# Three seven-product chunks in each up projection, with weight sums formed by adding transfers

## The chip, the cores and the metric

The kernel runs on one core of one Trainium2 chip. The metric is the device time of one execution in microseconds (us). A core has TensorE (PE in the profile, with its weight load as PEld), VectorE (DVE), ScalarE (ACT), GpSimd (POOL) and SyncE (SP), and 16 DMA engines that move data between the chip's main memory and the core's. SP and POOL issue most transfers here, each from a queue of its own that works strictly in order.

## The reference, cut to what matters

A decoder trunk of two layers on one sequence of 256 tokens, width 1024, in fp32. Each layer is half a SwiGLU, a token mixer, and another half SwiGLU; the mixers (delta and retention heads, then dilated and differential attention) are not touched by the change.

```
def swiglu(h, w_up, w_down):                    # w_up (1024, 5632), w_down (2816, 1024)
    gate, up = jnp.split(h @ w_up, 2, axis=-1)
    return (jax.nn.silu(gate) * up) @ w_down

for i in range(2):
    x = x + 0.5 * swiglu(rmsnorm(x, n1), wu1, wd1)
    x = x + mixer_i(rmsnorm(x, mix_norm[i]))
    x = x + 0.5 * swiglu(rmsnorm(x, n2), wu2, wd2)
return rmsnorm(x, final_norm)
```

So there are four feed-forward stages, each with an up projection and a down projection.

## The kernel before, in words

**Three products for one.** Every matrix operand is split into a rounded high part and the rest (`hi`, `lo`), and each matmul is done three times (hi·hi, hi·lo, lo·hi; `mm3`, lines 320 to 323). A weight reaches PE in blocks of 128 x 1024 numbers, 512 KB: `feed` (line 198) loads one from main memory on SP's queue, ACT casts it to `hi` (line 219), DVE subtracts to get `lo` (line 220). `feed` is called for at most four blocks ahead of the one that PE is at (`LOOKAHEAD`), and there are five buffers each for `w`, `hi` and `lo`.

**Chunks.** An up projection is cut into six chunks of columns: chunks 0 to 4 have 512 columns of the gate half and the same 512 of the up half, chunk 5 has 256 of each. The token axis has two halves t of 128, the inner axis eight k-tiles. A chunk done directly takes 8 blocks and 96 matmuls of 128x512, 12 to a block.

**Seven products.** Chunks 1 and 3 are done by the Strassen-Winograd scheme: inner axis and tokens are halved on one side, inner axis and the gate and up halves on the other, and seven products (P1 to P7) of quarter size stand for eight. Each product takes two blocks (p = 0, 1) of 6 matmuls, so a chunk takes 14 blocks and 84 matmuls. The sums of the inputs are formed once in each stage (`sums`); the sums of weights are formed for each chunk. With a, b, c, d for the weight quarters (0,0), (0,1), (1,0), (1,1), they are t = a+b, u = t+d, b+d, and u+c; in the up projection all four are DVE additions (`form`, line 180), two of each. The quarters stay in ten buffers named `raw`. Chunk 1 is interleaved with chunk 2 done directly, chunk 3 with chunk 4 (`PAIRS`, the list `SEVEN`, and `seven_and`): a product's two blocks of 6 matmuls, then mostly two blocks of 12. Chunks 0 and 5 are direct, at the two ends.

**The down projection** does its first eight k-tiles by seven products too, interleaved with the other 14 k-tiles of its first column half (`DOWN`, `seven_down`); the second column half of those 14 follows directly. Here t and b+d are formed while loading: a plain transfer of one quarter on SP (line 170), and then a transfer on POOL's queue that adds the other quarter to it in place (line 172, `accum_op`). Such a transfer is called an adding transfer below.

**What sets the order.** The program is written block by block; the framework then fixes an order of instructions for each engine, which the engine keeps. A `w` or `raw` load waits until the last reader of its buffer is done, and everything behind it on SP waits with it. In `feed`, loads of `raw` quarters are called a number of blocks ahead of their use (`LEAD`, `EARLY`).

Of the kernel before, what the change touches and what calls it, by code (L numbers as in the profile page):

```python
# [26 lines left out]
H = 4  # L27
# [8 lines left out]
LEAD, EARLY, RAW_BUFS = 4, 8, 10  # L36
# [4 lines left out]
PAIRS = ((1, 2), (3, 4))  # L41
# [4 lines left out]
def trunk(ctx, tc, a, out):  # L46
# [44 lines left out]
    def seven(w, cols, n, order, early=False, **between):  # L91

        kb = BLK // n

        def quarter(i, j, p):
            r0 = (4 * i + kb * p) * P
            return w[r0:r0 + kb * P, cols[j]:cols[j] + n].rearrange("(k p) c -> p k c", p=P)

        st = {}
        r = []  # L100
        for x in order:
            if x[0] == "P":
# [5 lines left out]
    def seven_up(w, c, mate):
        def cols(c):
            return (c * CW, FF + c * CW)  # L110

        gate, up = (cut([one(w, 0, 8, x)]) for x in cols(mate))
        return seven(w, cols(c), CW, SEVEN, G=gate, U=up)

    def up_runs(w, first=False):
        r, c = [], 0
        while c < 5:
            mate = dict(PAIRS).get(c)
            if mate is None:
                g, u = c * CW, FF + c * CW  # L120
                r += cut(([one(w, 0, 1, g), one(w, 1, 1, g), one(w, 2, 6, g)] if first and c == 0 else
                          [one(w, 0, 8, g)]) + [one(w, 0, 8, u)])
                c += 1
            else:
                r += seven_up(w, c, mate)
                c = mate + 1
        return r + cut([(0, 8, CW, [(w, 5 * CW, 256), (w, FF + 5 * CW, 256)])])
# [17 lines left out]
    stream = (up_runs(a["l0_ffn1_w_up"], True) + down_runs(a["l0_ffn1_w_down"])  # L145
              + cut(in0_runs(a["l0_w_in"]) + out_runs(a["l0_w_out"], 4))
              + up_runs(a["l0_ffn2_w_up"]) + down_runs(a["l0_ffn2_w_down"])
              + up_runs(a["l1_ffn1_w_up"]) + down_runs(a["l1_ffn1_w_down"])
              + cut(in1_runs(a["l1_w_in"]) + out_runs(a["l1_w_out"], 4))
              + up_runs(a["l1_ffn2_w_up"]) + down_runs(a["l1_ffn2_w_down"]))  # L150
# [7 lines left out]
    def load(x, p, st, quarter, n, early):  # L158
# [6 lines left out]
        if early:  # L165

            for nm, *src in {"P1": (("a", (0, 0)),), "P6": (("t", (0, 1), (0, 0)), ("d", (1, 1))),
                             "P7": (("b", (0, 1), (1, 1)),), "P2": (("c", (1, 0)),)}.get(x, ()):
                v = raw(nm + str(p)).rearrange("p (k n) -> p k n", n=n)
                nc.sync.dma_start(out=v, in_=quarter(*src[0], p))  # L170
                if src[1:]:
                    nc.gpsimd.dma_start(out=v, in_=quarter(*src[1], p), accum_op=ALU.add)
            return
        for nm, i, j in {"P1": (("a", 0, 0),), "P6": (("b", 0, 1), ("d", 1, 1)), "P2": (("c", 1, 0),)}.get(x, ()):
            nc.sync.dma_start(out=raw(nm + str(p)).rearrange("p (k n) -> p k n", n=n), in_=quarter(i, j, p))

    def form(x, p, st, early):

        def add(out, in0, in1):
            nc.vector.tensor_tensor(out=out, in0=in0, in1=in1, op=ALU.add)  # L180
# [17 lines left out]
    def feed():  # L198
        i = pos[1]
        while loaded[0] < len(stream) and loaded[0] <= i + (EARLY if stream[loaded[0]][-1] is True else LEAD):  # L200
            if isinstance(stream[loaded[0]][0], str):
                if spool[0] is None:
                    break
                load(*stream[loaded[0]])
            loaded[0] += 1
# [1121 lines left out]
```

## Time and profile before

| | us |
|---|---|
| runs | 1011.33, 1010.08, 1007.51 (median 1010.08) |
| the profiled execution | 1007.63 |
| its span, first to last instruction | 1005.8 |
| PE busy in it | 985.9 (98%) |
| DVE busy in it | 880.1 (88%) |
| ACT busy in it | 609.0 (61%) |
| third feed-forward stage, up projection (529.34 to 649.06) | 119.72 |
| the same, down projection (649.06 to 708.64) | 59.58 |

Busy shares are of the whole span. Matmuls are pipelined, so the duration of one (0.39 us) is longer than the distance to the next; the distances between starts tell the pace. The share of the DMA engines is the time that packets took, summed over 16 engines, and goes a little over 1 where packets overlap.

### The profile page before, as it was taken

What the parts mean: (1) busy time and instruction counts of PE and PEld (TensorE: products, weight loads), DVE (VectorE), ACT (ScalarE), POOL (GpSimd) and SP (SyncE); (2) the same over time, 40 slices, a digit from 0 to 9 for tenths busy, and PEclk for the clock granted to TensorE, in tenths of its full rate; (3) what the DMA queues carried; (4) which work ended last, traced back from release to release, by engine and by line L of the source; (5) the groups of instructions that cost most, each with busy time, mean ns of one, the idle gap of its engine ahead of it and who ended that gap; (6) DMA issues with size and microseconds to landing.
All of it is one profiled execution on the core that took longest, in us unless ns stands there. A gap on an engine that the chain in (4) does not pass through costs nothing.

```text
span 1005.8 us, 13951 instructions
## 1 busy us (share of the span) xinstructions
PE 985.9 (98%) x5076; PEld 812.9 (81%) x5076; DVE 880.1 (88%) x1191; ACT 609.0 (61%) x829; POOL 48.9 (5%) x56
## 2 busy tenths in 40 slices
PE   7999999999999999999999999999999999999997
PEld 6788878888777888888788888878877888888785
DVE  6999999679997699999979899998679879999994
ACT  6576666579543566666656566656556556666562
POOL 0000100100001000000000000100100000001000
PEclk9999999999999999999999999999999999999999
DMA  9665963765403577499267747935752566749731
GB/s 321 228 228 180 291 200 128 238 171 149 141 12 110 156 259 245 124 277 267 84 212 270 248 144 241 292 101 188 232 168 88 167 210 209 248 150 289 230 106 62
DMA packets 104708, 192.69 MB, mean 192 GB/s; under 512 B 6560, under 2 KB 16944, under 8 KB 104640
## 3 DMA queue, kind: packets, MB, share of 16 engines
q1 hardware_dynamic: 98752, 179.89, 55.1%
q0 software_dynamic: 5312, 11.30, 5.6%
q8 instruction: 40, 0.66, 0.3%
q10 hardware_dynamic: 576, 0.61, 0.2%
q14 instruction: 28, 0.23, 0.1%
HBM read 190.73 MB, written 1.05 MB: 191 GB/s over the span
## 4 chain that ended last, share of the span: by engine, by line
PE 89%; DVE 5%; ACT 2%; issue 1%; DMA 1%; POOL 1%; SPq 0%; POOLq 0%; ACTq 0%; DVEq 0%
PE p L322 7%; PE p L323 7%; PE p L321 7%; PE y L321 6%; PE y L323 6%; PE y L322 6%; PE gate L323 6%; PE gate L321 6%; PE gate L322 6%; PE up L321 4%; PE up L322 4%; PE up L323 4%; PE ca L321 2%; PE ca L322 2%; PE ca L323 2%; PE gtr L452 2%
## 5 line engine op out<-in xcount | busy, mean ns | idle before, releaser
L220 DVE TENSOR_TENSOR lo<-w,hi 128x1024 fp32r<-128x1024 f32 (+2 forms) x238 | 284.5, 1210 | 65.0 <-ACT hi L219 64.6
L219 ACT CAST hi<-w 128x1024 fp32r<-128x1024 f32 (+2 forms) x238 | 245.5, 1044 | 128.7 <-PE y L323 50.7
L219 ACT CAST hi<-raw 128x1024 fp32r<-128x1024 f32 x168 | 174.4, 1053 | 132.2 <-DVE raw L180 49.5
L220 DVE TENSOR_TENSOR lo<-raw,hi 128x1024 fp32r<-128x1024 f32 x168 | 201.6, 1218 | 15.4 <-ACT hi L219 14.0
L321 PE MATMUL gate<-hi,xT_hi 128*128 128x512 f32 x256 | 101.3, 400 | 2.1 <-ACT xT_hi L278 1.9
L323 PE MATMUL gate<-hi,xT_lo 128*128 128x512 f32 x256 | 101.0, 395 | 0.0
L322 PE MATMUL gate<-lo,xT_hi 128*128 128x512 f32 x256 | 100.7, 393 | 0.0
L180 DVE TENSOR_TENSOR raw<-raw 128x1024 f32<-128x1024 f32 x80 | 97.0, 1216 | 0.3
L321 PE MATMUL y<-hi,gT_hi 128*128 128x512 f32 x224 | 87.2, 392 | 1.8 <-ACT hi L219 1.8
L323 PE MATMUL y<-hi,gT_lo 128*128 128x512 f32 x224 | 87.4, 390 | 0.0
L322 PE MATMUL y<-lo,gT_hi 128*128 128x512 f32 x224 | 87.2, 389 | 0.0
L321 PE MATMUL p<-hi,fhP 128*128 128x512 f32 x192 | 75.2, 392 | 0.2
L322 PE MATMUL p<-lo,fhP 128*128 128x512 f32 x192 | 74.9, 390 | 0.1
L323 PE MATMUL p<-hi,flP 128*128 128x512 f32 x192 | 74.7, 389 | 0.0
L321 PE MATMUL up<-hi,xT_hi 128*128 128x512 f32 x192 | 74.7, 389 | 0.0
L322 PE MATMUL up<-lo,xT_hi 128*128 128x512 f32 x192 | 74.7, 389 | 0.0
L323 PE MATMUL up<-hi,xT_lo 128*128 128x512 f32 x192 | 74.7, 389 | 0.0
L321 PEld LDWEIGHTS gate<-hi,xT_hi 128*128 128x128 f32 x256 | 48.5, 190 | 12.3 <-ACT xT_hi L278 2.3
L323 PEld LDWEIGHTS gate<-hi,xT_lo 128*128 128x128 f32 x256 | 48.6, 190 | 10.3
L322 PEld LDWEIGHTS gate<-lo,xT_hi 128*128 128x128 f32 x256 | 48.7, 190 | 9.7
L321 PEld LDWEIGHTS y<-hi,gT_hi 128*128 128x128 f32 x224 | 41.7, 188 | 11.2 <-ACT hi L219 3.0
L323 PEld LDWEIGHTS y<-hi,gT_lo 128*128 128x128 f32 x224 | 42.1, 188 | 8.7
(322 smaller groups left out, 1868.0 us busy)
## 6 DMA issues: line engine op xcount, KB each, us to landing
w<-l_ffn_w_up SPq DMA_DIRECT2D x95, 512.0 KB, 4.2
raw<-l_ffn_w_up SPq DMA_DIRECT2D x64, 512.0 KB, 4.9
w<-l_ffn_w_down SPq DMA_DIRECT2D x56, 512.0 KB, 5.1
w<-l_w_in SPq DMA_DIRECT2D x50, 512.0 KB, 3.8
raw<-l_ffn_w_down SPq DMA_DIRECT2D x40, 512.0 KB, 6.5
w<-l_ffn_w_up SPq DMA_DIRECT2D x34, 256.0 KB, 4.8
raw<-l_ffn_w_down POOLq DMA_DIRECT2D x16, 512.0 KB, 9.9
w<-l_w_out SPq DMA_DIRECT2D x16, 512.0 KB, 3.6
```

What stands on the lines that cost most here:

```text
L180: nc.vector.tensor_tensor(out=out, in0=in0, in1=in1, op=ALU.add)
L219: nc.scalar.copy(out=hi[:, :k * n], in_=w[:, :k * n])
L220: nc.vector.tensor_tensor(out=lo[:, :k * n], in0=w[:, :k * n], in1=hi[:, :k * n].bitcast(F32), op=ALU.subtract)
L321: nc.tensor.matmul(ps, lhsT=xh, rhs=wh, start=start, stop=False, skip_group_check=more)
L322: nc.tensor.matmul(ps, lhsT=xh, rhs=wl, start=False, stop=False, skip_group_check=more)
L323: nc.tensor.matmul(ps, lhsT=xl, rhs=wh, start=False, stop=stop, skip_group_check=more)
L452: nc.tensor.transpose(ps[:, j * P:(j + 1) * P], gs[t][:, j * P:(j + 1) * P], ident)
```

## The change

Chunk 4 of each up projection, direct until now, is done by seven products as chunks 1 and 3 are; chunk 2 is cut into its gate half and its up half, and these and chunk 5 stand between the products of the three seven-product chunks, one block (M0 to M3) at a time: the gate half of chunk 2 in chunk 1, its up half in chunk 3, chunk 5 in chunk 4. Of the four weight sums three are now made by adding transfers in all seven-product chunks, up and down: t and b+d as in the down projection before, and u+c by a transfer that adds c to the buffer of u once P6's low part is made from it. Only u = t+d stays on DVE. The products' order changes (P3 before P7, both before P2), with the sums of the results rearranged to match. A block's own `w` load now comes ahead of the `raw` loads called with it, at most two `raw` loads are called with a block, and they are called 5 to 9 blocks ahead.

```
-PAIRS = ((1, 2), (3, 4))
+TRIPLE = ((1, "gate"), (3, "up"), (4, "last"))
+MATE, LAST = 2, 5
-LEAD, EARLY, RAW_BUFS = 4, 8, 10
+LEAD, RAW_BUFS = {"P1": 8, "P2": 5}, 10
-    SEVEN = ("P1", "G0", "G1", "P6", "G2", "G3", "P7", "U0", "U1", "P5", "U2", "U3", "P2", "P4", "P3")
-    DOWN = ("H0", "H1", "P1", "H2", "P6", "H3", "P7", "H4", "P5", "P2", "H5", "P4", "P3", "H6")
+    SEVEN = ("P1", "M0", "P6", "M1", "P5", "M2", "P3", "P7", "M3", "P2", "P4")
+    DOWN = ("H0", "H1", "P1", "H2", "P6", "H3", "P5", "H4", "P3", "P7", "H5", "P2", "P4", "H6")
...
-    def load(x, p, st, quarter, n, early):
+    def load(x, p, st, quarter, n):
...
+        for nm, *src in {"P1": (("a", (0, 0)),), "P6": (("t", (0, 1), (0, 0)), ("d", (1, 1))),
+                         "P7": (("b", (0, 1), (1, 1)),), "P2": (("c", (1, 0)),)}.get(x, ()):
+            v = raw(nm + str(p)).rearrange("p (k n) -> p k n", n=n)
+            nc.sync.dma_start(out=v, in_=quarter(*src[0], p))
+            if src[1:]:
+                nc.gpsimd.dma_start(out=v, in_=quarter(*src[1], p), accum_op=ALU.add)
...
         if x == "P6":
-            if not early:
-                st[f"t{p}"] = g["t"] = new()
-                add(g["t"], g["a"], g["b"])
             st[f"u{p}"] = g["u"] = new()
-            add(g["u"], g["t"], g["d"])
-        elif x == "P7" and not early:
-            add(g["b"], g["b"], g["d"])
-        elif x == "P4":
-            add(g["u"], g["u"], g["c"])
+            nc.vector.tensor_tensor(out=g["u"], in0=g["t"], in1=g["d"], op=ALU.add)
...
+        some = 0
+        while loaded[0] < len(stream) and loaded[0] <= i + LEAD.get(stream[loaded[0]][0], 9):
+            if isinstance(stream[loaded[0]][0], str):
+                if spool[0] is None or loaded[0] >= ends[0] or some == 2:
+                    break
+                some += 1
+                load(*stream[loaded[0]])
+            loaded[0] += 1
...
+        if stream[i][0] == "P6":
+            nc.gpsimd.dma_start(out=w.rearrange("p (k n) -> p k n", n=n), in_=stream[i][3](1, 0, stream[i][1]),
+                                accum_op=ALU.add)
...
-            while c < 6:
...
+            xs_run(gate, xT_hi, xT_lo, 0, 8)
+            xs_run(up, xT_hi, xT_lo, 0, 8)
+            chunk_out(0, gate, up, CW)
+            finish(sm)
+            for c, mate in TRIPLE:
+                seven_and(c, mate)
```

What this does to the order is shown at three places, all in the third feed-forward stage.

SP's queue from chunk 0 to the second seven-product chunk, before. `w` rows are blocks of chunks done directly, `raw` rows quarters of a seven-product chunk.

```order
L218 DMA w_5197<-l_ffn_w_up 128x2x512
L175 DMA raw<-l_ffn_w_up 128x2x512 x2
L218 DMA w_5215<-l_ffn_w_up 128x2x512
L218 DMA w_5291<-l_ffn_w_up 128x2x512
L175 DMA raw<-l_ffn_w_up 128x2x512 x4
L218 DMA w_5309<-l_ffn_w_up 128x2x512
L218 DMA w_5350<-l_ffn_w_up 128x2x512
L218 DMA w_5368<-l_ffn_w_up 128x2x512
L218 DMA w_5418<-l_ffn_w_up 128x2x512
L175 DMA raw<-l_ffn_w_up 128x2x512 x2
```

The same place after the change; w_5277 is M0 of chunk 1, w_5347, w_5401 and w_5481 are M1 to M3, and w_5575, w_5630, w_5684, w_5764 are M0 to M3 of chunk 3.

```order
L186 DMA w_5277<-l_ffn_w_up 128x2x512
L160 DMA raw<-l_ffn_w_up 128x2x512 x8
L186 DMA w_5347<-l_ffn_w_up 128x2x512
L186 DMA w_5401<-l_ffn_w_up 128x2x512
L186 DMA w_5481<-l_ffn_w_up 128x2x512
L186 DMA w_5575<-l_ffn_w_up 128x2x512
L160 DMA raw<-l_ffn_w_up 128x2x512
L186 DMA w_5630<-l_ffn_w_up 128x2x512
L160 DMA raw<-l_ffn_w_up 128x2x512
L186 DMA w_5684<-l_ffn_w_up 128x2x512
L160 DMA raw<-l_ffn_w_up 128x2x512 x2
L186 DMA w_5764<-l_ffn_w_up 128x2x512
```

Eight `raw` loads in one go (a, t, d, b, two of each) take the place of two and four, the rows behind them are c and then a of the next chunk, and the next row after the last one shown is `raw` x4: t and d of chunk 3, two of each.

POOL's queue in the third stage, before and then after; the rstd row is the reciprocal root of the stage's norm, L162 are the adding transfers into t and b, L203 those into u.

```order
L286 TENSOR_TENSOR rstd_3461<-rsq,mhalf 128x2
L172 DMA raw<-l_ffn_w_down 128x2x512 x4
L1055 DMA lamv<-lamv 128x256
```

```order
L270 TENSOR_TENSOR rstd_3500<-rsq,mhalf 128x2
L162 DMA raw<-l_ffn_w_up 128x2x512 x4
L203 DMA raw<-l_ffn_w_up 128x2x512 x2
L162 DMA raw<-l_ffn_w_up 128x2x512 x4
L203 DMA raw<-l_ffn_w_up 128x2x512 x2
L162 DMA raw<-l_ffn_w_up 128x2x512 x4
L203 DMA raw<-l_ffn_w_up 128x2x512 x2
L162 DMA raw<-l_ffn_w_down 128x2x512 x4
L203 DMA raw<-l_ffn_w_down 128x2x512 x2
L1036 DMA lamv<-lamv 128x256
```

Four adding transfers in a stage become 24, 18 of them in the up projection.

DVE's queue where the first seven-product chunk ends and the second begins, before: lo_5619 is chunk 1's last product, lo_5633 and the one behind w_5664 belong to chunk 3 and its companion.

```order
L220 TENSOR_TENSOR lo_5619<-raw,hi_5618 128x1024
L441 SCALAR_TENSOR_TENSOR g<-q,rstd_3461,s 128x512
L441 SCALAR_TENSOR_TENSOR g<-r,rstd_3461,s 128x512
L180 TENSOR_TENSOR raw<-raw 128x1024
L276 TENSOR_TENSOR gT_lo<-gtr,gT_hi 128x4x128
L180 TENSOR_TENSOR raw<-raw 128x1024
L276 TENSOR_TENSOR gT_lo<-gtr,gT_hi 128x4x128
L180 TENSOR_TENSOR raw<-raw 128x1024
L220 TENSOR_TENSOR lo_5633<-raw,hi_5632 128x1024
L220 TENSOR_TENSOR lo_5663<-w_5664,hi_5662 128x1024
```

The same place after: lo_5530 is the last block of chunk 1 (P4), lo_5550 and lo_5560 are the two blocks of P1 of chunk 3, lo_5574 is its M0, lo_5589 and lo_5616 are P6.

```order
L200 TENSOR_TENSOR lo_5519<-raw,hi_5518 128x1024
L416 TENSOR_TENSOR r<-r,p_5329 128x512
L200 TENSOR_TENSOR lo_5530<-raw,hi_5529 128x1024
L172 TENSOR_TENSOR raw<-raw 128x1024 x2
L200 TENSOR_TENSOR lo_5550<-raw,hi_5549 128x1024
L200 TENSOR_TENSOR lo_5560<-raw,hi_5559 128x1024
L425 SCALAR_TENSOR_TENSOR g<-u_5506,rstd_3500,s 128x512
L200 TENSOR_TENSOR lo_5574<-w_5575,hi_5573 128x1024
L200 TENSOR_TENSOR lo_5589<-raw,hi_5588 128x1024
L416 TENSOR_TENSOR q<-q,p_5329 128x512
L200 TENSOR_TENSOR lo_5616<-raw,hi_5615 128x1024
```

Both additions u = t+d of chunk 3 (L172 x2) stand ahead of the two blocks of P1, three blocks before the one that uses the first of them. The order is the same here in all four stages. In chunk 4 the two additions stand behind M0, in the down projection behind H2.

## Rows read from the trace of the kernel before

**Rows 1.** The page: engines' busy us and share; DMA queues: packets, MB, share.
```profile
PE 985.9 (98%) x5076; PEld 812.9 (81%) x5076; DVE 880.1 (88%) x1191; ACT 609.0 (61%) x829; POOL 48.9 (5%) x56
...
q1 hardware_dynamic: 98752, 179.89, 55.1%
q0 software_dynamic: 5312, 11.30, 5.6%
```
**Rows 2.** Stretches of the third stage: us, busy us of each engine, clock, DMA share, GB/s.
```profile
529.34:649.06 119.72, 119.72 (x554) 99.56 (x552) 114.57 (x124) 75.53 (x92) 6.43 (x5) 1.00 0.76 235
649.06:708.64 59.58, 59.08 (x266) 48.40 (x264) 51.35 (x59) 34.73 (x43) 0.00 (x0) 1.00 0.52 164
```
**Rows 3.** PE over time, third stage: start, us, line, operation, count.
```profile
529.34 0.39 PE L321 MATMUL gate<-hi,xT_hi 128*128 128x512 f32 x1
...
552.02 0.39 PE L321 MATMUL p<-hi,xT_hi 128*128 128x512 f32 x1
...
554.75 1.03 PE L452 MATMUL gtr<-ident,g 128*128 128x128 f32 x8
555.54 0.48 PE L321 MATMUL gate<-hi,xT_hi 128*128 128x512 f32 x1
```
**Rows 4.** DVE over time, third stage, chunk 1's end.
```profile
591.24 2.35 DVE L220 TENSOR_TENSOR lo<-raw,hi 128x1024 fp32r<-128x1024 f32 x2
593.51 0.68 DVE L432 TENSOR_TENSOR g<-q,p 128x512 f32<-128x512 f32 x1
594.10 2.35 DVE L220 TENSOR_TENSOR lo<-w,hi 128x1024 fp32r<-128x1024 f32 x2
```
**Rows 5.** Groups by line: count, busy us, mean ns, idle before and its releasers.
```profile
L219 ACT CAST hi<-raw 128x1024 fp32r<-128x1024 f32 x168 | 174.4, 1053 | 132.2 <-DVE raw L180 49.5 <-PE up L323 37.4 <-PE gate L323 12.8
L180 DVE TENSOR_TENSOR raw<-raw 128x1024 f32<-128x1024 f32 x80 | 97.0, 1216 | 0.3
```
**Rows 6.** DMA from 20 to 29 us, plain loads alone.
```profile
DMA packets 1870, 3.62 MB, mean 403 GB/s; under 512 B 108, under 2 KB 108, under 8 KB 1869
...
q1 hardware_dynamic: 1869, 3.61, 104.1%
```
**Rows 7.** DMA from 112 to 130 us, plain loads and adding transfers; GB/s in 40 slices.
```profile
GB/s 241 264 291 232 269 232 264 282 369 373 410 382 378 218 232 214 223 223 214 337 350 351 278 241 232 200 209 155 177 232 232 218 259 278 337 287 287 246 255 255
...
q0 software_dynamic: 932, 1.81, 56.1%
q1 hardware_dynamic: 1560, 3.00, 49.0%
```
**Rows 8.** The adding transfers (line 172): issue ns min/median/max, and issue to landing.
```profile
L172 POOL DMA_DIRECT2D raw<-l_ffn_w_down x16: 1195/1197/1402, 106.4 to 927.7; - x16
...
DMA to landing us min/median/max: 6.3/9.9/11.9
```
**Rows 9.** The plain raw loads of the down projection (line 170), issue to landing.
```profile
DMA to landing us min/median/max: 3.4/6.5/11.2
```
**Rows 10.** SP over time, start of the third stage.
```profile
529.75 0.88 SPq L175 DMA_DIRECT2D raw<-l_ffn_w_up  x2
531.88 3.43 SPq L218 DMA_DIRECT2D w<-l_ffn_w_up  x2
535.36 2.02 SPq L175 DMA_DIRECT2D raw<-l_ffn_w_up  x4
```
**Rows 11.** The kernel's start over time: SP, then PE.
```profile
0.74 0.86 SPq L258 DMA_DIRECT2D x_sb<-x  x2
...
9.45 0.63 PE L321 MATMUL gate<-hi,xT_hi 128*128 128x512 f32 x1
9.88 0.63 PE L322 MATMUL gate<-lo,xT_hi 128*128 128x512 f32 x1
...
34.11 0.39 PE L321 MATMUL p<-hi,xT_hi 128*128 128x512 f32 x1
```

More of the change, by code (lines that the diff above doesn't have):

```diff
@@ L102, in seven @@
             if x[0] == "P":
-                r += [(x, p, st, quarter, n, early) for p in range(4 // kb)]
+                r += [(x, p, st, quarter, n) for p in range(4 // kb)]
             else:
@@ L106, in seven @@
         return r
[L108 to L113, printed above, removed]
-    def up_runs(w, first=False):
[L116 to L127, printed above, removed]
+    def up_runs(w, first=False):
+        mates = {"gate": [one(w, 0, 8, MATE * CW)], "up": [one(w, 0, 8, FF + MATE * CW)],
+                 "last": [(0, 8, CW, [(w, LAST * CW, 256), (w, FF + LAST * CW, 256)])]}
+        r = cut(([one(w, 0, 1, 0), one(w, 1, 1, 0), one(w, 2, 6, 0)] if first else [one(w, 0, 8, 0)])
+                + [one(w, 0, 8, FF)])
+        for c, mate in TRIPLE:
+            r += seven(w, (c * CW, FF + c * CW), CW, SEVEN, M=cut(mates[mate]))
+        return r
     def down_runs(w):
-        return seven(w, (0, CW), CW, DOWN, True, H=cut([one(w, 8, KF - 8, 0)])) + cut([one(w, 8, KF - 8, CW)])
+        return seven(w, (0, CW), CW, DOWN, H=cut([one(w, 8, KF - 8, 0)])) + cut([one(w, 8, KF - 8, CW)])
     def in0_runs(w):
@@ L143, in out_runs @@
         return [one(w, k0, 4, c * CW) for k0 in (first, 4 - first) for c in (0, 1)]
[L145 to L150, printed above, removed]
+    stream, ends = [], []
+    for l, w_in, w_out, in_runs, out_first in ((0, a["l0_w_in"], a["l0_w_out"], in0_runs, 4),
+                                               (1, a["l1_w_in"], a["l1_w_out"], in1_runs, 4)):
+        for f in (1, 2):
+            stream += up_runs(a[f"l{l}_ffn{f}_w_up"], not stream) + down_runs(a[f"l{l}_ffn{f}_w_down"])
+            ends.append(len(stream))
+            if f == 1:
+                stream += cut(in_runs(w_in) + out_runs(w_out, out_first))
     ready = []
@@ L163, in raw, with form @@
             return st[nm]
[L165 to L180, printed above, removed]
+        for nm, *src in {"P1": (("a", (0, 0)),), "P6": (("t", (0, 1), (0, 0)), ("d", (1, 1))),
[4 more added lines that the diff above has]
+                nc.gpsimd.dma_start(out=v, in_=quarter(*src[1], p), accum_op=ALU.add)
+    def form(x, p, st):
         def new():
@@ L199, in feed @@
         i = pos[1]
[L200 to L205, printed above, removed]
         pos[1] += 1
@@ L479, in seven_and @@
-                product("P5", pc)
-                tt(r, pc, r, ALU.subtract)
-                xs_run(up, xT_hi, xT_lo, 4, 4)
-                next(spawn(turn(mate, [times(up[t], s2[t], t) for t in range(NT)], CW)))
+                xs_run(m, xT_hi, xT_lo, 2, 2)
+                product("P5", pc)
+                r = post("r")
+                tt(r, pc, q, ALU.subtract)
+                xs_run(m, xT_hi, xT_lo, 4, 2)
+                product("P3", pc, True)
+                u0 = post("u0")
+                tt(u0, pc, q, ALU.subtract)
@@ L483, in seven_and @@
+                product("P7", pd)
+                tt(r, r, pd, ALU.subtract)
+                xs_run(m, xT_hi, xT_lo, 6, 2)
+                if mate == "gate":
+                    kept.extend(silu(m[t], t, CW, "sq") for t in range(NT))
+                elif mate == "up":
+                    next(spawn(turn(MATE, [times(m[t], kept.pop(0), t) for t in range(NT)], CW)))
+                else:
+                    chunk_out(LAST, [p[:, :256] for p in m], [p[:, 256:] for p in m], 256)
                 product("P2", pa, True)
-                s0 = silu(pa, 0)
+                g0 = times(u0, silu(pa, 0), 0)
@@ L485, in seven_and @@
                 product("P4", pd, True)
[L486 to L511 removed]
+                tt(q, q, pd)
@@ L512, in seven_down @@
+                next(spawn(turn(c, [g0, times(r, silu(q, 1), 1)], CW)))
+            spool[0] = gpool
+            sm = spawn(sums(xT_hi, xT_lo))
+            gate = [pA("gate") for _ in range(NT)]
+            up = [pB("up") for _ in range(NT)]
+            xs_run(gate, xT_hi, xT_lo, 0, 8)
+            xs_run(up, xT_hi, xT_lo, 0, 8)
+            chunk_out(0, gate, up, CW)
+            finish(sm)
+            for c, mate in TRIPLE:
+                seven_and(c, mate)
             def seven_down(y):
@@ L564, in ffn @@
             spool[0] = None
+            ends.pop(0)
     def out_proj(oT_hi, oT_lo, nxt, first, need):
```

73 lines of the change are left out of this document (23 added, 50 removed).

## Prediction

> **What bounds the kernel now.** I read the page first: PE is busy 98% of the span and DVE 88% [rows 1], so time comes off only where PE does less, and only if nobody who feeds PE falls behind. Then the stretches of one feed-forward stage: in the up projection PE is busy for all of 119.72 us, DVE for 114.57, and the DMA engines show a share of 0.76 [rows 2]. The pace is in the starts: 12 matmuls of 128x512 lie between 552.02 and 554.75, 0.2275 us each, and eight transposes take 0.79 (554.75 to 555.54) [rows 3]. DVE makes two low parts in 2.27 us (591.24 to 593.51), 1.14 each, and a 512-wide sum in 0.59 [rows 4]. So PE is the bound, with DVE close beside it. The DMA rows I read last and they decide: in the before kernel transfers hide, and this change adds mostly transfers.
>
> **What PE loses.** One chunk of 96 matmuls becomes 84, in four stages: 48 matmuls by 0.2275 us, 10.9 us. All of it is on the path, since PE has no idle time in these stretches. Against the profiled execution (1007.63 us, 2.45 under the median of the runs) that is 996.7; put on the median, 999.2.
>
> **What DVE, ACT and POOL get.** DVE loses 48 sums of weights and gains 24 low parts (chunk 4 takes 14 blocks, not 8) and 20 sums of 512 columns: -54.7 + 27.4 + 11.8 = -15.5 us, 3.9 a stage, where PE loses 2.7. So DVE stays beside PE and is costed at nothing; if that cover went, what DVE runs over would show in the stretch behind chunk 4, where its work and PE's are nearly equal. ACT gains 24 casts at 1.05 us [rows 5], 25 us on an engine that is 61% busy: nothing. The idle time of ACT behind DVE's sums of weights, 49.5 us [rows 5], goes, and costs PE nothing now. POOL issues 80 more adding transfers at 1.2 us [rows 8], 96 us on a queue that is 5% busy. In that queue each transfer waits for what it adds to; the ones behind are needed later, so nothing is charged for the queue itself.
>
> **What the DMA engines get.** A plain 512 KB load takes 1.30 us at the 403 GB/s that loads alone reach [rows 6]. An adding transfer is dearer. From 112 to 130 us the engines were full: 3.00 MB plain at 403 GB/s fill 7.4 of the 18 us, and 10.6 are left for 1.81 MB, 3.06 us for 512 KB; shared out by their shares (56.1 against 49.0, scaled to 18 us) it is 2.77. I take 2.9. The slices show it as well: 220 to 260 GB/s where both run, up to 410 where one does [rows 7].
>
> A seven-product chunk with its companion now needs 14 plain loads (a, t, d, b, c twice, four M blocks) and 6 adding transfers: 18.2 + 17.4 = 35.6 us. PE needs 132 matmuls and eight transposes for it: 30.0 + 0.8 = 30.8. So through the three chunks the engines fall behind by 4.8 us a chunk; only what is loaded during chunk 0 carries them. In the down projection it is 24 plain and 6 adding, 48.6 us, beside 59.6 of PE [rows 2]: hidden.
>
> **Where it first runs out.** In the new order of DVE the two sums u = t+d of chunk 3 stand ahead of both low parts of P1. Behind them waits all of DVE, and PE waits for those low parts; the buffers of PE's lead end exactly there, with P4 of chunk 1. PE gets to that P1 at 552.02 - 529.34 = 22.7 us for chunk 0 [rows 3], plus 30.8: 53.5 us after the stage's start. Its second matmul needs the low part, so the second t must have landed by 53.5 + 0.2 - 2 x 1.14 = 51.4.
>
> Until then the engines must move, from the first `raw` load on (0.4 us into the stage, as now [rows 10]; the stage's earlier w blocks are in): a, t, d, b twice (8), M1 to M3, M0 (4), c twice (2), M1 and M2 (2), a twice (2), M3 (1), t, d, t (3): 22 plain loads, and 8 adding transfers (t, b, u twice, and t twice): 28.6 + 23.2 = 51.8. They end at 52.2 if the engines never pause. The quickest adding transfer took 6.3 us to land [rows 8], of which 1.2 is issue and 2.9 transfer; the other 2.2 make it 54.4: 3.0 us late. With the median landing of 9.9, which is that of adding transfers beside plain loads, it is 6.6 late. The median holds some waiting behind another adding transfer, which the sum has already, so I take the middle, 4.8 us. A plain load beside others also lands in 6.5 us in the median and not in its fastest 3.4 [rows 9]; that is inside these ends.
>
> In the first stage there is no head start: x is 2 loads more, chunk 0 is 8 and M0 one, so 33 plain, 42.9, and 23.2, from 0.74 us: 66.8, landed at 69.0. It is needed at 34.1 [rows 11] + 30.8 + 0.2 - 2.3 = 62.8. Late by 6.2 to 9.8; 8.0 in the middle.
>
> Later in a stage it holds: in chunk 4 the sums stand behind M0, so the next t is needed 31.6 + 5.4 - 1.1 = 35.9 us after the last, and comes 35.6 after it. The wait at chunk 3 pays for all of the stage, by 0.3 us.
>
> **The sum.** 1007.6 - 10.9 + 3 x 4.8 + 8.0 = 1019.1 for the profiled execution, and 1021.6 on the median. I forecast 1021 us, slower by 1.1%. The low ends (3 x 3.0 + 6.2 = 15.2) give 1014 on the median, the high ends (3 x 6.6 + 9.8 = 29.6) 1029.
>
> **A rule weighed.** Rows 8 show 6.3 us for the quickest adding transfer of 512 KB and 9.9 for the median. The Trainium skill (DMA: Bandwidth & Descriptors, "Anatomy of one DMA") puts a transfer issued from GpSimd at about 2.0 us plus its bytes over 436 GB/s, 3.2 us here as an estimate, and makes no dearer case of one that adds. By it nothing would be late. The trace does not agree, by a factor of two to three, and I go by the trace.
>
> **Rivals.** *An adding transfer is no dearer to the engines than a plain one* and its slow landing is only latency. For it: only 16 were seen, beside other traffic, and PE never waited on them. Then a chunk needs 20 x 1.30 = 26.0 us, under 30.8, and the second t has landed by 0.4 + 30 x 1.30 + 2.2 = 41.6. All of the gain stays: 999 us, faster. Against it: the slices of rows 7, which fall to half whenever such transfers run. Chance 0.20.
>
> *The wait is just about the gain.* If the engines run at 410 GB/s, the best slice, and 2.77 us an adding transfer, the sum to the second t is 50.3 and the lateness 1.5; the first stage's 64.4 gives 4.5. Waits of 9.0 against 10.9: 1008 us on the median, no change. Chance 0.22.
>
> *The engines stay behind.* If each chunk behind the first wait is late by the 4.8 us that it lacks, and not covered by the first wait, one more such wait in each stage makes 1041; this is decided by whether DVE can rebuild its lead in chunk 3, and the 0.3 us above say how close that is. For it: the balance of 35.6 to 30.8. Against: each wait gives the engines its own length. Chance 0.08.
>
> *The clock of PE falls in the wait.* At the kernel's start, after PE has been idle, its matmuls start 0.43 us apart (9.45 to 9.88) [rows 11], and not 0.2275, its lower level. If the 12 matmuls of P1 go at that pace after each wait, it costs 2.4 us four times: 1031. Against: the granted clock is 1.00 through the stages [rows 2], but they hold no wait of this length, so no row decides it. The Trainium skill (TensorE: Matmul & The Clock Gate, Part 1) has such a fall after an idle stretch; no stretch of this trace tests it in the middle of the work. Chance 0.08.
>
> **Chances and range.** The forecast has 0.42. About 0.5% (5 us) is what a measurement of this kernel can tell from no change. Faster by more: the first rival, 0.20. Within it: the second, 0.22. Slower: the forecast and the last two, 0.58. The forecast's own range is 1012 to 1030. For 8 in 10 it must reach into both sides: 998 to 1033, which leaves out the lower part of the first rival and the longest waits.
>
> **What would show it.** Right: in each up projection one PE wait of 3 to 7 us some 53 us after its start (longer in the first), released by DVE's low part, with DVE itself waiting ahead of the sums u for a DMA into `raw`; the up projections' DMA share at 0.95 or over; the down projections unchanged within 1 us. Matmuls fewer by 48. Wrong: no idle time of DVE ahead of those sums, up projections of 117 us, adding transfers that land in 6 us amid plain loads; or waits spread over every chunk.

## The result, and the profile after

The changed kernel takes 1063.81 us (median of 4 runs, 1059.82 to 1064.75) against 1008.99 for the kernel before beside it: 1.053 times the time, 95% interval 1.0508 to 1.0556. Slower was forecast, but 1021 us with a range to 1033; the loss is 55 us and not 12. The profiled execution took 1064.75 us, its span 1063.0.

First the page of the changed kernel: busy time by engine, PE's granted clock in 40 slices, DMA queues, and the shares of the chain that ended last.

```profile
PE 997.4 (94%) x5028; PEld 814.2 (77%) x5028; DVE 867.8 (82%) x1187; ACT 638.2 (60%) x857; POOL 144.3 (14%) x136
...
PEclk9989999999999999899999989999999999899999
...
q1 hardware_dynamic: 105280, 192.47, 52.9%
q0 software_dynamic: 27072, 53.25, 27.3%
...
PE 65%; DMA 14%; DVE 12%; issue 4%; ACT 3%; SPq 1%; POOL 0%; POOLq 0%; DVEq 0%; ACTq 0%
```

Against [rows 1] there are 48 matmuls fewer, and yet PE is busy 11.5 us longer. The span grew by 57.2 us: PE's idle time by 45.7 (19.9 to 65.6) and its busy time by 11.5. The matmuls taken away are worth 10.9, so PE was busy 22.4 us longer than the matmuls left ask for; most of that is matmuls at the lower clock (below). The same stretches as in [rows 2], the third stage's up and down projection:

```profile
559.26:687.62 128.36, 121.19 (x537) 100.04 (x536) 108.88 (x121) 81.46 (x98) 25.75 (x21) 0.96 1.04 296
687.62:752.93 65.31, 61.98 (x270) 49.83 (x268) 54.08 (x62) 36.09 (x45) 4.85 (x4) 0.97 0.74 208
```

The up projection is 8.6 us longer and has the DMA engines full (share 1.04), the down projection 5.7 longer. In both the clock is no longer 1.00. What PE waited for, in the whole execution (us in total, times, longest):

```profile
PE p L306 <- DVE lo L200: 28.2, 8, 8.5
PE y L305 <- ACT hi L199: 9.1, 8, 1.3
PE gtr L436 <- DVE g L425: 7.2, 4, 2.5
```

25.2 of the 28.2 us are the wait forecast: one in each stage at P1 of chunk 3 (8.54, 6.53, 4.66 and 5.45 us), the rest is in the down projections. Here it is in the third stage, first DVE over time, then PE (start, us, line, operation; in brackets the idle time before and its releaser):

```profile
610.46 1.22 DVE L200 TENSOR_TENSOR lo<-raw,hi 128x1024 fp32r<-128x1024 f32 x1
616.12 1.23 DVE L172 TENSOR_TENSOR raw<-raw 128x1024 f32<-128x1024 f32 x1 [4.44 <-issue]
619.43 1.23 DVE L172 TENSOR_TENSOR raw<-raw 128x1024 f32<-128x1024 f32 x1 [2.09 <-DMA raw<-l_ffn_w_up]
620.58 2.35 DVE L200 TENSOR_TENSOR lo<-raw,hi 128x1024 fp32r<-128x1024 f32 x2
```
```profile
616.80 0.39 PE L305 MATMUL p<-hi,xT_hi 128*128 128x512 f32 x1
621.85 0.80 PE L306 MATMUL p<-lo,xT_hi 128*128 128x512 f32 x1 [4.66 <-DVE lo L200]
622.45 0.63 PE L307 MATMUL p<-hi,xT_lo 128*128 128x512 f32 x1
622.87 0.63 PE L305 MATMUL p<-hi,xT_hi 128*128 128x512 f32 x1
```

DVE stands twice ahead of u = t+d until t has landed (the second time released by the DMA into `raw`; for the first the profile names no releaser, `issue`), and both low parts of P1 are queued behind. PE came to this P1 57.5 us after the stage's start (616.80 - 559.26), and the second u could start at 60.2 (619.43). When PE goes on, matmuls start 0.43 us apart, not 0.2275. The granted clock in four pieces of that time (us, busy us and counts of PE, PEld, DVE, ACT, POOL, then clock, DMA share, GB/s) tells why: 0.50, which is 1.2 GHz of 2.4, behind the wait, and 1.00 in the stretch that starts 6.65 us after it.

```profile
616.80:621.85 5.05, 0.39 (x2) 0.00 (x0) 2.96 (x4) 2.09 (x2) 1.20 (x1) 0.91 1.04 161
621.85:626.70 4.85, 4.85 (x11) 3.71 (x12) 4.85 (x6) 1.04 (x1) 0.54 (x1) 0.50 1.07 305
626.70:628.50 1.80, 1.80 (x9) 1.65 (x8) 1.21 (x2) 1.55 (x3) 1.27 (x2) 0.71 1.23 312
628.50:632.00 3.50, 3.50 (x19) 2.88 (x18) 3.42 (x5) 2.56 (x4) 0.60 (x1) 1.00 0.96 154
```

Two kinds of waits were not forecast. At chunk 1 the transposes of chunk 0's result wait for DVE's g, which stands behind chunk 1's sums u (7.2 us, in three of the four stages). In each down projection y waits twice for ACT's casts (9.1 us; 1.8 before).

### The profile page after: what moved, and what is told of

Its sections match the earlier page's. It is cut to its first block, busy times and chain, and to the rows that moved or that the text cites. A ratio compares the mean times of both kernels' runs of the same rounds, so it can differ in the third digit from the quotient of the medians.

```text
span 1063.0 us, 14242 instructions
## 1 busy us (share of the span) xinstructions
PE 997.4 (94%) x5028; PEld 814.2 (77%) x5028; DVE 867.8 (82%) x1187; ACT 638.2 (60%) x857; POOL 144.3 (14%) x136
## 3 DMA queue, kind: packets, MB, share of 16 engines
q1 hardware_dynamic: 105280, 192.47, 52.9%
q0 software_dynamic: 27072, 53.25, 27.3%
## 4 chain that ended last, share of the span: by engine, by line
PE 65%; DMA 14%; DVE 12%; issue 4%; ACT 3%; SPq 1%; POOL 0%; POOLq 0%; DVEq 0%; ACTq 0%
DMA raw<-l_ffn_w_up 12%; PE p L306 7%; PE p L307 7%; PE p L305 7%; PE y L306 5%; DVE lo L200 5%; PE y L307 5%; PE y L305 5%; PE mate L305 3%; PE mate L307 3%; PE mate L306 3%; PE ca L305 2%; PE ca L306 2%; ACT hi L199 2%; PE ca L307 2%
## 5 line engine op out<-in xcount | busy, mean ns | idle before, releaser
L199 ACT CAST hi<-raw 128x1024 fp32r<-128x1024 f32 x224 | 232.3, 1053 | 122.1 <-DVE raw L172 45.4
L200 DVE TENSOR_TENSOR lo<-raw,hi 128x1024 fp32r<-128x1024 f32 x224 | 269.0, 1220 | 19.4 <-ACT hi L199 16.4
L162 POOL DMA_DIRECT2D raw<-l_ffn_w_up x48 | 58.1, 1210 | 237.2 <-DMA raw<-l_ffn_w_up 118.9
L306 PE MATMUL p<-lo,xT_hi 128*128 128x512 f32 x144 | 60.4, 419 | 25.2 <-DVE lo L200 25.2
L305 PE MATMUL mate<-hi,xT_hi 128*128 128x512 f32 x192 | 77.1, 402 | 0.0
L307 PE MATMUL mate<-hi,xT_lo 128*128 128x512 f32 x192 | 76.4, 398 | 0.0
L306 PE MATMUL mate<-lo,xT_hi 128*128 128x512 f32 x192 | 75.7, 394 | 0.0
L172 DVE TENSOR_TENSOR raw<-raw 128x1024 f32<-128x1024 f32 x32 | 39.1, 1222 | 43.2 <-issue 22.0
L305 PE MATMUL p<-hi,xT_hi 128*128 128x512 f32 x144 | 59.4, 413 | 0.0
L307 PE MATMUL p<-hi,xT_lo 128*128 128x512 f32 x144 | 59.4, 413 | 0.0
```

What stands on the lines that cost most here:

```text
L172: nc.vector.tensor_tensor(out=g["u"], in0=g["t"], in1=g["d"], op=ALU.add)
L305: nc.tensor.matmul(ps, lhsT=xh, rhs=wh, start=start, stop=False, skip_group_check=more)
L306: nc.tensor.matmul(ps, lhsT=xh, rhs=wl, start=False, stop=False, skip_group_check=more)
L307: nc.tensor.matmul(ps, lhsT=xl, rhs=wh, start=False, stop=stop, skip_group_check=more)
```

## The experiments

Ratios are to the kernel before on the same chip, with 95% intervals. The first four ask what the second transfers cost.

**e1_plain.** The edit:
```
-  nc.gpsimd.dma_start(out=v, in_=quarter(*src[1], p), accum_op=ALU.add)
+  nc.gpsimd.dma_start(out=v, in_=quarter(*src[1], p))        (and the same for c)
```


> The 96 adding transfers become plain ones of the same bytes from the same queue, each written over what it would have been added to (the sums of weights are left out). Theory A (an adding transfer holds the DMA engines more than twice as long as a plain one, and that is what makes the t sums late): a seven-product chunk then needs 20 transfers by 1.30 us = 26.0 us beside 30.8 of PE, the waits ahead of u and the PE waits behind them are gone, the granted clock stays at 1.00: 1009.0 - 10.9 = 998 us, within 995 to 1004, landing of those transfers under 6 us in the median. Rival B (the second transfer of the same place is what costs, whether it adds or not: 54 MB more, one queue more): the waits at chunk 3 stay at more than half of 25.2 us, over 1035 us.

Measured: 1023.92 us, 1.0146 (1.0107 to 1.0185). Same bytes, same queue, 40 us less. The queue's row:
```profile
q0 software_dynamic: 14784, 53.25, 14.5%
```
53.25 MB held the 16 engines for 14.5% of 1022.2 us, 1.46 us for 512 KB; adding, it was 27.3% of 1063.0 us. Without the 2.91 MB of other transfers on this queue (0.8% of 1013.7 us in e2_skip) that is 2.94 us, and the forecast's 2.9 was right. The plain transfers also came in about half as many packets (14784 against 27072), but that is not the reason: SP's plain loads in the changed kernel, in packets no larger than the adding ones (105280 for 192.47 MB), took 52.9%, which is 1.53 us for 512 KB. No PE wait at P1 of chunk 3 is left and landing fell from 9.8 to 6.4 us in the median; B falls. But 1024 is not 998: something else costs 26 us.

**e2_skip.** Both `nc.gpsimd.dma_start(..., accum_op=ALU.add)` deleted; the sums lack a summand.


> The 96 adding transfers are left out, and with them the second summand of t, b+d and u+c. This is the floor of the change: what fewer matmuls give when no second transfer is there. Both A and B: 998 us (995 to 1003), no PE wait over 1 us inside an up projection. Over 1008 us would speak for rival C: something else in the change costs (the order of the products, the longer lead of the loads, DVE's order), with PE waits that stand at the same places.

Measured: 1017.65 us, 1.0078 (1.0051 to 1.0105): the rival C, slower than before without any second transfer. The third stage shows where:
```profile
533.50:650.24 116.74, 116.74 (x538) 96.72 (x537) 108.43 (x121) 81.61 (x98) 1.54 (x1) 1.00 0.74 252
650.24:713.70 63.46, 60.16 (x269) 48.48 (x268) 53.83 (x61) 36.02 (x45) 0.00 (x0) 1.00 0.45 149
```
The up projection has its gain (119.72 to 116.74); the down projection lost 3.9 us, 2.8 of them idle (0.50 before, 3.30 here).

**e3_order.** u is queued on DVE behind the newest low part:
```
+  with tc.issue_after(low[0]):
       nc.vector.tensor_tensor(out=g["u"], in0=g["t"], in1=g["d"], op=ALU.add)
```


> The sum u is queued on DVE behind the newest low part (P1's second low part for chunk 3's first u), so P1 no longer waits for t; loads and adding transfers are as in the changed kernel. Theory A (the DMA engines lack some 5 us a chunk): the wait at P1 of chunk 3 goes (25.2 us and the slow matmuls behind it, 10 us), but the engines have not caught up by it, and PE waits of 2 us or more appear at P6 of chunk 3 or in chunk 4 and the down projection; 1035 to 1055 us. Rival O (only the in-order place of u on DVE is at fault, the transfers would be in time for P6): no new wait over 1 us behind chunk 3, 1028 us or less.

Measured: 1044.40 us, 1.0338 (1.0305 to 1.0372). As A has it, the waits at P1 go and others come, though not at P6: they stand at the transposes of chunk 1's result in chunk 3, in the first stage also in chunk 4.
```profile
PE gtr L439 <- DVE g L428: 16.0, 5, 4.1
PE y L308 <- ACT hi L201: 10.4, 8, 1.7
```
DVE's order chose which of PE's work had to wait; the late t is the cause. Moving u is still worth 19 us.

**e4_t_dve.** t on DVE, up and down; b+d and u+c by transfers:
```
+  nc.vector.tensor_tensor(out=g["t"], in0=g["a"], in1=g["b"], op=ALU.add)
+  nc.gpsimd.dma_start(out=g["b"]..., in_=quarter(1, 1, p), accum_op=ALU.add)
```


> t = a+b is formed on DVE again (b loaded plain, 24 up and 8 down sums of 1.22 us more on DVE); b+d and u+c stay adding transfers, 64 in all and none ahead of u. Theory A: a chunk needs 12 plain and 4 adding transfers, 12 x 1.30 + 4 x 2.9 = 27.2 us, under PE's 30.8: no wait ahead of u, 998 to 1008 us. Rival D (with 907 us of work DVE is too full beside a PE of some 990): waits on DVE's low parts and g of under 1 us each, spread over the chunks, 1010 to 1025 us. Rival B: still over 1035.

Measured: 1034.09 us, 1.0240 (1.0209 to 1.0270). A's number fails by 26 us though its waits are gone: what is left is DVE's, y waiting for a cast behind DVE's sums, 4.2 us at the start of each down projection (16.8 in all). The cause is rival D's, a DVE too full, but as one long wait a stage and not as short ones spread over the chunks, and 9 us above D's range.

The next four take that apart, and do the other half of the change alone.

**e5_t_up.** As e4, in the up projections alone (down has t by a transfer).


> As e4_t_dve, but t goes to DVE in the up projections alone; the down projections form it by adding transfers again, as before the change. Theory T (at the start of each down projection DVE, in its order, has the sums of gT, their low parts, the last low parts of gT and the sums u to do all at once, because chunk 4 with its wide transposes now ends the up projection; ACT's casts stand behind those): without the two t sums there the wait of 4.2 us shrinks to the three of e2_skip (1.3, 0.95 and 0.75), with fewer slow matmuls behind them: 1034 - 4 x 2 = 1026 us, 1022 to 1029. Rival S (e4 loses time in the up projections, where b+d and u+c still add): 1032 or more.

Measured: 1030.76 us, 1.0208 (1.0179 to 1.0238). The waits in the down projection are the three expected (1.63, 0.95, 0.74), the time is 2 us above T's range: the up projections keep 1.7 us of waits a stage, at chunk 4's start.

**e6_early.** In chunk 4, behind P7 (shortened):
```
+  if mate == "last":
+      down_sums.append(spawn(sums(gT_hi, gT_lo, down_forms)))
```


> As e5_t_up, and the sums of gT for the down projection are started in chunk 4 behind its P7, five blocks earlier, with all else in its order. Theory T: the waits of y on ACT's casts (9 to 10 us in the four stages) and the slow matmuls behind them go: 1026 - 13 = 1013 us, 1008 to 1018. Rival N (the new order of the down projection's blocks is at fault, P5 ahead of P7 and P3 ahead of P2): no more than 3 us better than e5_t_up.

Measured: 1031.00 us, 1.0215 (1.0186 to 1.0243). T falls as it was put: the waits only moved, from y (1.8 us for casts in all, 10.4 in e5) to p (11.8, 4.2 in e5). From 654 to 677 us of the third stage, chunk 4's end and the down projection's start, DVE's timeline has no idle time, so starting the sums earlier only moves what waits.

**e7_down.** DOWN and the results in the old order.


> As e5_t_up, but the down projection's blocks and results come in the order that they had before the change (P6, P7, P5, P2, P4, P3). Theory T: the same as e5_t_up within 4 us. Rival N: the waits of y on ACT's casts go and it is 10 us or more faster than e5_t_up.

Measured: 1027.26 us, 1.0180 (1.0150 to 1.0211), 3.5 us better than e5. N falls: the order of the blocks is worth 3.5 us, not the loss.

**e8_pairs_add.** The kernel before, its `load`, `form` and `feed` replaced by the changed kernel's.


> The kernel before with its own order and two seven-product chunks a stage, in which only the way of forming t, b+d and u+c is changed: by adding transfers, with the changed kernel's leads (64 more of them in place of 48 sums of DVE; no fewer matmuls). Theory A: a pair of chunks needs 18 plain and 6 adding transfers, 18 x 1.30 + 6 x 2.9 = 40.8 us, beside 180 matmuls, 41 us: nearly even, so small waits at the first u of a pair, 1008 to 1022 us, taken 1014. If the adding transfers hurt whatever the pace that the order asks for: 1035 or more. If they are hidden at this pace: 1009.

Measured: 1028.09 us, 1.0184 (1.0150 to 1.0218), 6 above the range. The sums' half of the change, with the changed kernel's order of loads, loses 19 us alone, with DVE at 821.3 us, 59 less than before. PE waits 8.4 us for g at transposes and 8.6 us for ACT's casts of the sums of gT. So relieving DVE by adding transfers did not pay here even where the sum for the engines came out even; what the order of loads has in it no run shows.

Then the rest of e2's loss, the clock, and two other places for the sums.

**e9_no_forms.** e2_skip without (and without `finish(sm)`)
```
-  sm = spawn(sums(gT_hi, gT_lo))
```


> As e2_skip (no second transfers), and the sums of gT that the down projection's products need are left out too (they take the sums of x of the up projection instead). Theory V (at the start of the down projection DVE's and ACT's own work is the bound: two wide sums, four narrow ones, four low parts, 7.2 us of DVE, come on top of chunk 4's end, where DVE has no lead): the waits of e2_skip there (13 us in the four stages) and the slow matmuls behind them (up to 4.7 us) go: 1017.7 - 15 = 1003 us, 999 to 1007, and the full gain of 10.9 us nearly stands. Rival W (the waits come from the order of the blocks, the buffers of w or the loads): the waits stay, 1013 or more.

Measured: 995.19 us, 0.9865 (0.9837 to 0.9894). The waits of the down projections are gone, the whole gain stands and 4 us more:
```profile
524.90:641.64 116.74, 116.74 (x537) 96.72 (x536) 108.71 (x122) 81.54 (x98) 1.54 (x1) 1.00 0.74 251
641.64:700.30 58.66, 58.66 (x268) 48.72 (x267) 47.24 (x51) 34.58 (x41) 0.00 (x0) 1.00 0.49 161
```
So the loss of e2 hangs on the sums of gT, 53.83 us of DVE's work in the down projection against 47.24. The kernel before makes the same sums and has 0.50 us of idle time there. Their last low part, in the kernel before and then in e2:
```profile
660.74 0.68 DVE L276 TENSOR_TENSOR flP<-keep,fhP 128x512 fp32r<-128x512 f32 x1
```
```profile
673.94 0.69 DVE L254 TENSOR_TENSOR flP<-keep,fhP 128x512 fp32r<-128x512 f32 x1
```
That is 11.7 us after the start of the down projection before, and 23.7 in e2. That chunk 4 leaves DVE without a lead, with no work done ahead, is read from these rows; no run changes the lead alone.

**e10_warm.** Ahead of chunk 3 (shortened):
```
+  for _ in range(20):
+      nc.tensor.matmul(warm, lhsT=xT_hi[:, 0, :P], rhs=xT_hi[:, 0:2, :]..., start=True, stop=True)
```


> The changed kernel with 20 more matmuls of 512 columns, whose result nobody reads, on PE between P4 of chunk 1 and P1 of chunk 3, in the place of 4.55 us of the wait there (18.2 us of added PE work in the four stages, less than the 25.2 us waited). Theory K (the idle time itself brings the clock down, and the 12 to 16 matmuls behind it pay 2.6 us a time): the waits shrink to 4.0, 2.0, 0.1 and 0.9 us, the matmuls behind them run at 0.2275 us in the last two stages at least, and the time falls by 5 to 10 us, to 1054 to 1059, though PE does more. Rival (the slow matmuls behind the wait have another cause, or the work only moves the wait): 1062 or more.

Measured: 1071.38 us, 1.0609 (1.0571 to 1.0647): K's forecast missed. In the third stage, which starts at 563.6 here:
```profile
593.55 1.97 PE L439 MATMUL gtr<-ident,g 128*128 128x128 f32 x8 [4.45 <-DVE g L428]
...
624.48 4.70 PE L459 MATMUL warm<-xT_hi 128*128 128x512 f32 x20
```
```profile
624.52 1.23 DVE L173 TENSOR_TENSOR raw<-raw 128x1024 f32<-128x1024 f32 x1 [2.72 <-DMA raw<-l_ffn_w_up]
```
The second t is in 60.9 us after the stage's start (60.2 in the changed kernel); but chunk 1's wait was 4.45 us instead of 2.51, so PE came to P1 only then, and the 4.55 us were added to work that no longer waited. (In the first stage the wait at P1 did shrink as expected, from 8.54 to 3.76 us.) Why chunk 1's t was later is open. By its time it decides nothing on the clock; but with PE busy right up to P1 in the third stage, the granted clock behind it reads 1.00 from 624.40 to 632.00, where the changed kernel had 0.50, and that agrees with K.

**e11_pool.** All four sums as `nc.gpsimd.tensor_tensor`, every quarter loaded once.


> The changed kernel with all four sums of weights formed by GpSimd's own adds (112 of 128x1024) in place of adding transfers and of DVE's sums u; each quarter is loaded once, plain. The price of such an add is in no row: bounds are DVE's 1.22 us for the same shape and, for 8 sums a chunk to keep pace with 30.8 us of PE, 3.85. Under that bound theory A expects no wait in the up projections (12 plain loads a chunk, 15.6 us) and, with 39 us less on DVE, about half of the waits at the start of the down projections: 1000 to 1012 us. If a sum takes over 3.85 us, or GpSimd's and DVE's work slow each other: 1030 or more, with u late again.

Measured: 1240.81 us, 1.2297 (1.2261 to 1.2332). There are 128 sums, not the 112 of the expectation. A sum of P6 (t, u or b+d) takes GpSimd 3.17 us, under the bound of 3.85, but DVE's low parts from `raw` take 1.76 (1.22 in the changed kernel):
```profile
L171 POOL TENSOR_TENSOR raw<-raw 128x1024 f32<-128x1024 f32 x96 | 302.6, 3168 | 253.7 <-DVE lo L201 228.5 <-DVE keep L392 13.2 <-DMA raw<-l_ffn_w_up 9.5
```
```profile
L201 DVE TENSOR_TENSOR lo<-raw,hi 128x1024 fp32r<-128x1024 f32 x224 | 390.2, 1757 | 28.9 <-ACT hi L200 25.3
```
DVE was slowed beside GpSimd's sums, the second case of the expectation; what a sum takes GpSimd beside an idle DVE no run shows. The Trainium skill (SBUF — State Buffer, "SBUF: two separate sides") says that a DVE operation with two SBUF inputs and a GpSimd operation that reads SBUF exclude each other; on DVE's side these rows agree (1220 to 1757 ns).

**e12_triple_dve.** The same with `nc.vector`: the new order alone.


> The new order with three seven-product chunks, but all four sums of weights on DVE, each quarter loaded once, no adding transfer: the change of the order alone. DVE has 108.4 us of work in an up projection of e2_skip (116.7 us long); 18 more sums of 1.14 us make 128.9, so each up projection should last 129 us or more, with PE waiting on low parts all through it, and the down projections 2 to 6 us longer: 1017.7 + 49 + 8 to 24, so 1066 to 1090 us. If the sums fit into DVE's idle time (the time of the third product saved stands): 1025 or less.

Measured: 1094.90 us, 1.0851 (1.0819 to 1.0883), 5 above the range. With DVE's sums a third seven-product chunk costs more than with transfers: PE spares 2.7 us a chunk, DVE needs 8 sums by 1.23.

**e13_stall.** e9_no_forms, for P1's first block of chunk 3 (shortened; the edit also fixes the order of these low parts and P1's on DVE):
```
+  for _ in range(8):
+      nc.vector.tensor_tensor(out=lo, in0=w, in1=hi.bitcast(F32), op=ALU.subtract)
```


> e9_no_forms (no second transfers, no sums of gT; PE waits nowhere in its stages) with one low part on DVE repeated eight times more, that of P1's first block of chunk 3: 9.1 us more of DVE ahead of P1 in each stage and nothing else changed, above all no transfer. It measures by itself what such a wait costs. Theory K (idle time itself brings the granted clock down): PE waits 3 to 9 us in the four places, and PE's busy time rises from 973.5 by 8 to 16 us, 2 to 4 a wait, with matmuls 0.43 us apart behind each wait. Rival (the slow matmuls of the changed kernel came from the transfers beside them): PE's busy time stays within 2 us of 973.5, matmuls 0.2275 apart behind the waits.

Measured: 1039.34 us, 1.0304 (1.0259 to 1.0348). PE is busy 983.2 us, 9.7 more for the same matmuls. In the third stage, PE and then the clock:
```profile
602.52 0.63 PE L440 MATMUL gtr<-ident,g 128*128 128x128 f32 x4 [2.36 <-DVE g L429]
609.55 0.80 PE L310 MATMUL p<-lo,xT_hi 128*128 128x512 f32 x1 [6.40 <-DVE lo L207]
610.14 0.63 PE L311 MATMUL p<-hi,xT_lo 128*128 128x512 f32 x1
610.57 0.63 PE L309 MATMUL p<-hi,xT_hi 128*128 128x512 f32 x1
```
```profile
603.10:609.50 6.40, 0.05 (x1) 0.00 (x0) 6.33 (x8) 0.58 (x1) 0.00 (x0) 0.57 0.01 3
609.50:612.00 2.50, 2.45 (x6) 1.97 (x7) 2.50 (x3) 0.00 (x0) 0.00 (x0) 0.50 0.53 137
612.00:614.50 2.50, 2.50 (x8) 1.98 (x7) 2.50 (x3) 1.05 (x1) 0.00 (x0) 0.55 0.95 311
614.50:617.00 2.50, 2.50 (x13) 2.04 (x12) 1.56 (x2) 1.65 (x3) 0.00 (x0) 1.00 0.79 237
```
With the DMA engines at 0.01 during the wait, the clock falls all the same, and K is shown: idle time of PE does it without any adding transfer. Against the text of the expectation something else did change: each stage has a second wait that e9 has not, 2.36 us at transposes, 0.63 us of work ahead of the long one (9.4 us in the four stages). The pause measured here is both together.

**e14_stall5.** The same with `range(5)`.


> As e13_stall with five repeats, 5.7 us more of DVE: shorter waits, 1 to 5 us. Theory K: PE's busy time still rises by 4 to 12 us, less than in e13_stall; a wait under 1 us, if any is left, is followed by matmuls 0.2275 us apart. Rival: no rise.

Measured: 1022.48 us, 1.0137 (1.0094 to 1.0179). The third stage:
```profile
593.74 0.63 PE L440 MATMUL gtr<-ident,g 128*128 128x128 f32 x4 [2.36 <-DVE g L429]
596.51 0.79 PE L310 MATMUL p<-lo,xT_hi 128*128 128x512 f32 x1 [2.15 <-DVE lo L207]
```
The waits are 2.36 and 2.15 us (in e13 2.36 and 6.40), again with 0.63 us of transposes between, and PE's busy time is 983.3, as in e13: against the expectation, the shorter pause costs as much busy time as the longer. What a single wait of 2 us costs it does not show.

**e15_t4.** t of chunk 4 by a transfer again.


> As e5_t_up, but t of chunk 4 comes by an adding transfer (t of chunks 1 and 3 stays on DVE). e5_t_up's waits in the up projection, 1.7 us a stage, stand at the start of chunk 4, where DVE has the sums t and u beside chunk 3's results. Theory V (DVE's amount of work there is the bound): they go, and chunk 4's 35.6 us of transfers are carried by the 3.6 us that chunks 1 and 3 each leave over: 1030.8 - 4 x 2.3 = 1022 us, 1018 to 1026. Theory A as the stricter rival (any chunk with six adding transfers is late): a wait of 2 us or more at chunk 4's first u, 1031 or more.

Measured: 1037.51 us, 1.0292 (1.0254 to 1.0330), 6.8 us slower than e5: the stricter rival. One chunk with six adding transfers is late again: in the third stage DVE stands 2.09 and 1.84 us ahead of chunk 4's two sums u for the DMA, and PE waits at the transposes behind (11.9 us in the four stages):
```profile
638.96 0.67 PE L444 MATMUL gtr<-ident,g 128*128 128x128 f32 x4 [3.63 <-DVE g L433]
```

## Why the prediction was wrong

The spans of the profiled executions make a ladder: before 1005.8; e9 994.1 (the third product saved, nothing late); e2 1013.7 (+19.6, the sums of gT on DVE); e1 1022.2 (+8.5, second transfers, plain); after 1063.0 (+40.8, adding). So the third product is worth 11.7 us, the sums of gT behind chunk 4 cost 19.6 where the forecast had nothing, and the second transfers cost 49.3 where it had 22.4. (Left out in another order, the parts could divide otherwise.)

- **What PE loses, 10.9 us:** right; e9 has 11.7 with the down projection's small waits gone too.
- **An adding transfer at 2.9 us, and the engines short by some 5 us a chunk:** right (2.94; share 1.04). The Trainium skill's estimate of 3.2 us from issue to landing (DMA: Bandwidth & Descriptors, "Anatomy of one DMA") does not hold for adding transfers: the row below (the 64 into t and b) has 5.9 at the least and 9.6 in the median.
```profile
DMA to landing us min/median/max: 5.9/9.6/14.2
```
- **Where it first runs out:** place, releaser and DVE's order right. 22.4 us were forecast, 25.2 measured: 2.8 us too few. That the size came so near was in part luck: in the third stage 4.8 us were forecast and 4.66 came, but PE was at P1 57.5 us after the stage's start and not 53.5, held up by the wait at chunk 1 and the slow matmuls behind it, and the second u could start at 60.2, where the forecast had t landed by 54.4 to 58.0 (56.2 in the middle). Both were 4.0 us late.
- **Later in a stage it holds:** chunk 4 has no such wait, as said. But only chunk 3's t was timed. Chunk 1's t, loaded from the stage's start on, was late too (DVE idle for 3.15 us ahead of the first u there, at 577.34), and through g it stopped PE's transposes.
- **DVE "costed at nothing", down "hidden":** failed; in the ladder this term, put at nothing, is 19.6 us. The text named the stretch behind chunk 4 as the place where a lost cover would show, and put no price there. DVE's total fell, by 12.3 us where 15.5 were forecast; but ACT's idle time behind DVE's sums of weights, which was to go (49.5 us), is still 45.4, and at that seam, where the down projection follows on chunk 4, the sums of gT meet a DVE with 53.83 us of work in 63.46 (e2) and no lead. In e4 and e12 more DVE work came out as more PE waits, in e6 an earlier start only moved them, and e8, which had less of it, bought with adding transfers and the new order of loads, lost all the same.
- **The rival of the clock, at 0.08:** it was the case, and its place in the sum was the second failure: it stood as an alternative, and so at nothing in the forecast, though it came behind all four forecast waits. The 10 us behind each of them:
```profile
76.74:86.74 10.00, 10.00 (x38) 7.87 (x39) 9.44 (x11) 5.31 (x7) 2.41 (x2) 0.76 1.00 247
428.88:438.88 10.00, 10.00 (x39) 8.01 (x40) 9.69 (x11) 5.35 (x8) 2.41 (x2) 0.78 1.03 261
621.85:631.85 10.00, 10.00 (x36) 8.11 (x37) 9.32 (x11) 5.00 (x7) 2.41 (x2) 0.71 1.06 255
928.16:938.16 10.00, 10.00 (x40) 8.02 (x41) 10.00 (x12) 5.74 (x8) 2.41 (x2) 0.83 1.06 264
```
By the clock of these rows that is 9.2 us lost (10 us times what each lacks to 1.00, an estimate), so its price of 2.4 us four times was right. What is left of the 22.4 us lies in part behind waits that were not forecast. (In the down projection of e2's third stage the clock reads 1.00 and PE's busy time is still 1.5 us more than in e9, so a part is not the clock; what it is no run shows.) The Trainium skill (TensorE: Matmul & The Clock Gate, Part 1) has a fall after idle time; e13 agrees.
- **The other rivals:** "no dearer" falls with e1 (2.94 us against 1.46); "just about the gain" had waits of 9.0 us, and 25.2 came; "the engines stay behind" put one more such wait in each stage, and none came in chunk 4.

The difference to the forecast adds up: span +57.2 against the +11.5 of the sum (1019.1 - 1007.6); 45.7 us too few, of which 22.4 are PE's longer busy time, 20.5 idle time at other places (45.7 - 25.2), 2.8 the wait's size. The parts overlap in cause: without adding transfers (e1) 25.4 us of the idle and 15.4 of the busy time go together.

Not settled: how the 8.5 us between e2 and e1 divide between bytes and the order "first transfer, then second" (e1 still waits 5.3 us for chunk 1's g, in chunk 3).

No version was found that beats the kernel before: e9 is faster only because it leaves work out, and in the divisions tried DVE with ACT's casts behind it, GpSimd and the DMA engines each failed to carry the third chunk's sums.

## What to carry to other kernels

Work taken from a full engine and given to the DMA engines has a price there: here 512 KB cost them 2.94 us when it adds and 1.46 when it doesn't; set that against the pace of each stretch, and ask for every first use in it, not one. A forecast wait of PE is not its length alone: the matmuls behind it may run at half clock, as behind all the waits of 4.66 us and more here, and that belongs in the sum and not among the alternatives. And where two stretches meet, look for an engine that has no lead and gets a burst of its own work: a lower total says nothing there.

## What the runs showed of the hardware

- An adding transfer holds the DMA engines twice as long as a plain one of the same bytes: 2.94 us for 512 KB against 1.46 on the same queue (e1) and 1.53 on SP's, in packets no larger, in the same trace. Its issue takes POOL 1.20 us and not 0.72 (e1).
- A pause of PE of 2.36 and 2.15 us, 0.63 us of transposes between, was followed by as much added busy time as one of 2.36 and 6.40 (e14 and e13: 983.3 and 983.2 us busy, 973.5 without). The length of a wait alone does not tell whether the clock falls. Behind two waits for g in the changed kernel, 2.48 us in the second stage and 2.51 in the third, it stayed at 1.00 in the first case and fell in the second:
```profile
393.57:398.57 5.00, 5.00 (x25) 4.11 (x26) 5.00 (x6) 3.01 (x4) 1.39 (x2) 1.00 1.07 317
587.30:592.30 5.00, 5.00 (x20) 4.45 (x21) 5.00 (x7) 3.39 (x5) 1.39 (x2) 0.71 1.08 330
```
- Beside GpSimd's own adds DVE's low parts from `raw` took 1.44 times as long in the mean (1757 ns in e11 against 1220 in the changed kernel).
